# Low parts of the first weight groups and of the shifted operand, and the rotations of keys and queries, issued on VectorE instead of GpSimd

## The chip, the cores and the metric

The kernel runs on one core of a Trainium2 chip. The metric is the device time of one execution in microseconds (us). A core has five engines, each with its own queue of instructions: TensorE (PE in the rows; its weight loads are PEld), VectorE (DVE), ScalarE (ACT), GpSimd (POOL) and SyncE (SP), which issues most of the DMAs.

## The reference, cut to what matters

One step of a hybrid encoder layer, for a prompt of 1024 frames and a sample of 64 frames with 512 cached ones, in float32. The input is normalized, scaled and shifted by the conditioning vector; one combined projection feeds two mixers, a latent attention and a gated linear recurrence; their outputs go through an output projection, and an MLP follows.

```python
h = rms_norm(x, g_norm1) * (1 + scale1) + shift1
proj = h @ w_in
c_q, c_kv, k_rope_raw, gq, gk, gv, g_lr, g_r = jnp.split(proj, split_points, axis=-1)
# latent attention: q and k get a per-head RMS norm, then the last 64 columns are rotated
q = jnp.concatenate([q[..., :QK_NOPE], rope(q[..., QK_NOPE:], q_pos)], axis=-1)
k = jnp.concatenate([k[..., :QK_NOPE], rope(k[..., QK_NOPE:], k_pos)], axis=-1)
# rope, on the halves x1, x2 of the 64 columns:
concatenate([x1 * cos - x2 * sin, x2 * cos + x1 * sin])
# gated linear recurrence over chunks of 64 frames (gla_recurrence)
x = x + gate1 * (concatenate([a_out, b_out]) @ w_out)
h2 = rms_norm(x, g_norm2) * (1 + scale2) + shift2
x = x + gate2 * (square(relu(h2 @ w_up)) @ w_down)
```

## The kernel before

**Products.** Each float32 operand of a large product is split into a high part, a rounded copy that ScalarE casts, and a low part, the operand minus the high part. `mm3` (L93 to L95) then makes three products: high by high, and each high by the other's low part. `split` (L101, L102) makes both parts of an operand; the engine of the subtraction is its last argument. In names, `hh` and `hl` are the high and low part of the normalized input `hf`, `wh` and `wl` those of a weight group, which arrives in a buffer `raw`.

**Tiling and stages.** The 1088 frames lie along the columns, in three chunks of 384, 384 and 320; the 1024 features lie along 8 tiles of 128 partitions, indexed by `k` or `kt`. At the start, `scales` sums the squares of a chunk (L331) and scales `hf` with the result (L379). The weight groups A0 and A1 (columns of the recurrence's queries and keys) come first, in eight units of 128x512, and `split_first` (L309) makes their low parts. `qk` multiplies chunk after chunk with A0 and A1 into `gqk` (L498, L508). `shifts` adds the shift to `hf`: for an even `k`, ScalarE writes `hh` (L478) and VectorE `hl` (L479); for an odd `k`, VectorE adds the shift in place (L476) and `split` makes both parts. Two later groups of weights, B0 and B1, are split at L213 and L105 in units of 128x528; when a low part is done its `raw` is free for the load of a later unit. L511 and L514 add the shift's share to `gqk`.

The recurrence follows (L560 to L800 or so): per tile of 128 frames TensorE transposes at L573, VectorE computes gates and sums, and GpSimd products of decays and operands at L660, L668 and L706. Then comes the latent attention: `keys_values` makes normalized keys and values for 13 tiles of frames, `queries` the queries for 9, and `attend` the attention. Tables of cosines and sines, `tabk` and `tabq` (`rotary_table`), are loaded and scaled at L824. In `keys_values` the raw rotary key is multiplied by both halves of the table into `ra` and `rt` and combined into `R`; the low part `kl` (L888) and the rotated keys `kr` (L895) follow transpositions on TensorE. `queries` forms products `qa` and `qt`, combines them into `qr` (L926, L927), and transposes `qn` (L938) and `qr` (L945). Powers for the norms run on GpSimd (L121, L351, L877, L930).

**What sets the order.** The stages are generators that yield an estimated cost and a condition, and `interleave` takes turns among them; from the order in which instructions are issued that way, a scheduler makes the queue of each engine. Each engine then runs its queue strictly in order, and waits on semaphores for data and for buffers. So an instruction that goes to another engine can also move its neighbours in several queues.

Of the kernel before, what the change touches and what calls it, by code (L numbers as in the profile page):

```python
# [36 lines left out]
def f32(ap):  # L37
    return ap.bitcast(F32)
# [33 lines left out]
def layer(ctx: ExitStack, tc: tile.TileContext, I, O):  # L72
# [202 lines left out]
    with ExitStack() as sctx:  # L275
# [26 lines left out]
        LO = ((DVE, POOL), (POOL, POOL))  # L302

        def split_first(hf, j):
            for u in (2 * hf, 2 * hf + 1):
                wh, wl = groups[GROUPS[j][0]]
                hi, lo, raw = wh[:, 2 * u:2 * u + 2], wl[:, 2 * u:2 * u + 2], first.pop((j, u))
                mm = ACT.copy(hi, raw)
                m2 = LO[hf][j].tensor_tensor(out=lo, in0=raw, in1=f32(hi), op=ALU.subtract)  # L309
                if hf == 0:  # L310
                    tc.keep_in_program_order(mm)
                    tc.keep_in_program_order(m2)
            done.add(f"half {hf} {j}")
# [7 lines left out]
        def scales(c):  # L321
# [8 lines left out]
            for n in (4, 2, 1):  # L330
                mm = (POOL if n == 4 and c == 2 else DVE).tensor_tensor(out=sq[:, 0:n, :cn], in0=sq[:, 0:n, :cn],  # L331
                                                                   in1=sq[:, n:2 * n, :cn], op=ALU.add)
                if c == 0:
                    tc.keep_in_program_order(mm)
# [125 lines left out]
        def shifts():  # L460
# [8 lines left out]
            for c in range(3):  # L469
                c0, cn = CHUNKS[c]  # L470
                yield 2000, 0, has(f"qk {c}")
                for k in range(KT):
# [8 lines left out]
                    if k % 2:  # L481
                        split(h["h"][:, k, c0:c0 + cn], h["l"][:, k, c0:c0 + cn], hf[:, k, c0:c0 + cn], POOL)
# [338 lines left out]
    def rotary_table(tab, w):  # L821
        SP.dma_start(tab, I["k_rope_tab"].rearrange("p t (c d) -> p t c d", d=64))
        t = tab.rearrange("p t c d -> p (t c) d")
        POOL.tensor_tensor(out=t, in0=t, in1=grow[:, w:w + 1].broadcast_to([P, 16, 64]), op=ALU.mult)  # L824
# [23 lines left out]
    def keys_values(lh, ll, ki, tab, n, kv, slot):  # L848
# [8 lines left out]
        POOL.tensor_tensor(out=a[:n, 0], in0=kraw[:n, ki], in1=tabk[:n, tab, 0], op=ALU.mult)  # L857
        POOL.tensor_tensor(out=t_[:n, 0], in0=kraw[:n, ki], in1=tabk[:n, tab, 1], op=ALU.mult)
        DVE.tensor_tensor(out=R[:n, 0, :, 0:32], in0=a[:n, :, 0:32].broadcast_to([n, 2, 32]),
                          in1=t_[:n, :, 32:64].broadcast_to([n, 2, 32]), op=ALU.subtract)  # L860
        POOL.tensor_tensor(out=R[:n, 0, :, 32:64], in0=a[:n, :, 32:64].broadcast_to([n, 2, 32]),
                           in1=t_[:n, :, 0:32].broadcast_to([n, 2, 32]), op=ALU.add)
# [37 lines left out]
    def queries(i, ch, cl_, n, tab):  # L900
# [26 lines left out]
        POOL.tensor_tensor(out=qr[:n, :, :, 32:64], in0=half(a, 32), in1=half(t_, 0), op=ALU.add)  # L927
# [915 lines left out]
```

## Time and profile before

| what | value |
|---|---|
| median of 3 runs | 1406.49 us (1406.09 to 1408.61) |
| profiled execution, its own time | 1403.91 us |
| its span in the trace | 1402.1 us |
| TensorE busy | 1340.1 us, 96% |
| VectorE busy | 890.4 us, 64% |
| ScalarE busy | 656.1 us, 47% |
| GpSimd busy | 183.8 us, 13% |

The span runs from the first to the last instruction that the profiler recorded in one execution; positions in the rows below are us from its start. A busy share says how much of the span an engine worked, not whether somebody waited for it; for that the rows give the idle time ahead of an instruction in brackets, with what ended it.

### The profile page before, as it was taken

To read this page: it belongs to the slowest core of one execution; us is meant where nothing else is said; L and a number is where in the kernel's file an instruction comes from. 1 tells how busy PE (TensorE), PEld (TensorE's weight loads), DVE (VectorE), ACT (ScalarE), POOL (GpSimd) and SP (SyncE) were. 2 spreads that over 40 slices of the span, in tenths; PEclk is the share of its full clock that TensorE was granted. 3 is DMA by queue.
4 is the path that set the end of the run, shared out by engine and by line. 5 is a ranking of instruction groups with operands and counts; after the bars stand their busy time and mean duration, and the time that the engine had idled before them with its cause. 6 is when DMAs were issued, how large, how long until landed. Compare 5 with 4: busy or idle time off the path is not lost.

```text
span 1402.1 us, 26363 instructions
## 1 busy us (share of the span) xinstructions
PE 1340.1 (96%) x10014; PEld 1254.8 (89%) x10014; DVE 890.4 (64%) x1965; ACT 656.1 (47%) x1623; POOL 183.8 (13%) x317
## 2 busy tenths in 40 slices
PE   6988889997999999999999999999999999999998
PEld 5888778886876778899998999999999999999998
DVE  5688777336546665665689766566555866774554
ACT  5465454334326565563386454454444343433342
POOL 3155445213122220100000000000000000000000
PEclk9999999999999999999999999999999999999999
DMA  9320021384344532073324543443348764543440
GB/s 345 115 73 9 16 73 47 112 238 120 100 130 124 172 108 77 26 219 115 107 85 135 191 158 133 140 158 133 112 157 285 280 227 152 188 122 97 126 128 33
DMA packets 165592, 188.15 MB, mean 134 GB/s; under 512 B 16814, under 2 KB 116442, under 8 KB 165466
## 3 DMA queue, kind: packets, MB, share of 16 engines
q1 hardware_dynamic: 158010, 180.90, 40.3%
q10 hardware_dynamic: 7456, 5.57, 1.2%
q8 instruction: 79, 1.29, 0.4%
q14 instruction: 47, 0.39, 0.1%
HBM read 132.97 MB, written 53.46 MB: 133 GB/s over the span
## 4 chain that ended last, share of the span: by engine, by line
PE 78%; DVE 10%; DMA 4%; ACT 3%; POOL 2%; issue 2%; SPq 0%; DVEq 0%; POOLq 0%; ACTq 0%
PE mm L93 13%; PE mm L94 13%; PE mm L95 13%; PE g L95 5%; PE g L93 5%; PE g L94 5%; PE mm L964 3%; PE tp L93 3%; PE tp L95 3%; PE tp L94 3%; PE g L991 2%; PE mm L166 2%; DMA raw<-in_w_in 1%; PE tp L1001 1%; DVE ST L725 1%
## 5 line engine op out<-in xcount | busy, mean ns | idle before, releaser
L101 ACT CAST opers<-quad 128x512 fp32r<-128x512 f32 x112 | 69.5, 620 | 184.5 <-PE mm L95 146.8
L102 DVE TENSOR_TENSOR opers<-quad,opers 128x512 fp32r<-128x512 f32 x112 | 77.3, 690 | 114.5 <-ACT opers L101 114.5
L95 PE MATMUL mm<-opers 128*128 128x272 f32 x448 | 128.9, 288 | 0.0
L93 PE MATMUL mm<-opers 128*128 128x272 f32 x448 | 128.5, 287 | 0.3 <-DVE e L1775 0.3
L94 PE MATMUL mm<-opers 128*128 128x272 f32 x448 | 128.3, 286 | 0.0
L93 PE MATMUL mm<-ah,wh 128*128 128x272 f32 x424 | 122.2, 289 | 3.3 <-ACT wh L101 2.2
L94 PE MATMUL mm<-al,wh 128*128 128x272 f32 x424 | 121.5, 287 | 0.0
L95 PE MATMUL mm<-ah,wl 128*128 128x272 f32 x424 | 121.4, 288 | 0.0
L93 PE MATMUL mm<-hh,wh 128*128 128x384 f32 (+2 forms) x264 | 90.6, 346 | 0.7 <-ACT hh L101 0.7
L94 PE MATMUL mm<-hl,wh 128*128 128x384 f32 (+2 forms) x264 | 87.6, 333 | 0.0
L95 PE MATMUL mm<-hh,wl 128*128 128x384 f32 (+2 forms) x264 | 87.2, 331 | 0.0
L93 PEld LDWEIGHTS mm<-opers 128*128 128x128 f32 x448 | 84.7, 189 | 0.5 <-issue 0.5
L95 PEld LDWEIGHTS mm<-opers 128*128 128x128 f32 x448 | 84.2, 188 | 0.0
L94 PEld LDWEIGHTS mm<-opers 128*128 128x128 f32 x448 | 84.0, 188 | 0.0
L93 PEld LDWEIGHTS mm<-ah,wh 128*128 128x128 f32 x424 | 79.8, 188 | 4.4 <-ACT wh L101 2.6
L94 PEld LDWEIGHTS mm<-al,wh 128*128 128x128 f32 x424 | 79.7, 188 | 0.0
L95 PEld LDWEIGHTS mm<-ah,wl 128*128 128x128 f32 x424 | 79.5, 188 | 0.0
L102 DVE TENSOR_TENSOR opers<-ru,opers 128x544 fp32r<-128x544 f32 x108 | 77.7, 720 | 2.2 <-ACT opers L101 2.0
L101 ACT CAST opers<-ru 128x544 fp32r<-128x544 f32 x108 | 69.4, 643 | 13.1 <-PE mm L95 11.7
L101 ACT CAST wh<-ru 128x512 fp32r<-128x512 f32 x67 | 41.3, 617 | 67.5 <-PE g L94 24.5
L102 DVE TENSOR_TENSOR wl<-ru,wh 128x512 fp32r<-128x512 f32 x67 | 46.1, 691 | 36.3 <-ACT wh L101 36.0
L93 PE MATMUL mm<-wh,hh 128*128 128x264 f32 (+3 forms) x216 | 66.0, 306 | 1.6 <-ACT wh L213 1.6
(410 smaller groups left out, 4370.0 us busy)
## 6 DMA issues: line engine op xcount, KB each, us to landing
ru<-u_d SPq DMA_DIRECT2D x108, 272.0 KB, 2.8
raw<-in_w_ada SPq DMA_DIRECT2D x40, 512.0 KB, 3.9
ru<-in_w_up SPq DMA_DIRECT2D x32, 512.0 KB, 4.0
quad<-in_w_down SPq DMA_DIRECT2D x16, 1024.0 KB, 6.5
u_d<-st SPq DMA_DIRECT2D x60, 272.0 KB, 2.1
u_d<-sc SPq DMA_DIRECT2D x45, 272.0 KB, 2.2
raw<-in_w_in SPq DMA_DIRECT2D x22, 256.0 KB, 3.5
x<-in_xo_T SPq DMA_DIRECT2D x8, 544.0 KB, 5.2
```

What stands on the lines that cost most here:

```text
L93: PE.matmul(out, lhsT=ah, rhs=bh, start=first, stop=False, skip_group_check=more)
L94: PE.matmul(out, lhsT=ah, rhs=bl, start=False, stop=False, skip_group_check=more)
L95: PE.matmul(out, lhsT=al, rhs=bh, start=False, stop=last, skip_group_check=more)
L101: ACT.copy(hi, src)
L102: eng.tensor_tensor(out=lo, in0=src, in1=f32(hi), op=ALU.subtract)
L166: mm = PE.matmul(acc[32 * j:32 * j + 32, 0:256], lhsT=scT[:, k, :], rhs=was[k][:, 256 * j:256 * (j + 1)], start=(k == 0), stop=(k == KT - ...
L725: DVE.copy_predicated(ST[:n, :, :n].rearrange("p c (b r h) -> p c b r h", r=2, h=hf)[:, :, :, 1], masks[:n, mlv, :n // 2].rearrange("p (o ...
L964: PE.matmul(sp[:n, :w], lhsT=x[:, hd, :n], rhs=y[:, hd, :w], start=(j == 0), stop=(j == 4))
L991: PE.matmul(op[:n, 0:P], lhsT=pt[:kw, k, :n], rhs=kvs[kt // 4].v[:kw, kt % 4, hd], start=(kt == 0), stop=(kt == nkt - 1))
L1001: PE.transpose(tp[:kw, k, :n], pr[k0 // 4][:n, P * k:P * k + kw], ident[:n, :n])
```

## The change

Instructions of six kinds, all on GpSimd before, are issued on VectorE: the low parts of A0 and A1 that were GpSimd's (six of eight, L309); the first addition of squares of chunk 2 (L331); the low parts of the shifted operand for odd `k` (twelve, at L102); the scaling of both rotary tables (L824); three of the four instructions that rotate a key tile (L857, L858, L861); and the second half of a rotated query tile (L927). On GpSimd stay the products of the recurrence and the powers. The arithmetic is the same. Two lines go, so that what is line N before is line N - 2 after, from L303 on.

```diff
--- before.py
+++ after.py
@@ -299,14 +299,12 @@
                     _, a, b = GROUPS[j]
                     SP.dma_start(first[j, u], w_in_cols(a, b)[2 * u * P:2 * u * P + 2 * P].rearrange("(k p) n -> p k n", p=P))
 
-        LO = ((DVE, POOL), (POOL, POOL))
-
         def split_first(hf, j):
             for u in (2 * hf, 2 * hf + 1):
                 wh, wl = groups[GROUPS[j][0]]
                 hi, lo, raw = wh[:, 2 * u:2 * u + 2], wl[:, 2 * u:2 * u + 2], first.pop((j, u))
                 mm = ACT.copy(hi, raw)
-                m2 = LO[hf][j].tensor_tensor(out=lo, in0=raw, in1=f32(hi), op=ALU.subtract)
+                m2 = DVE.tensor_tensor(out=lo, in0=raw, in1=f32(hi), op=ALU.subtract)
                 if hf == 0:
                     tc.keep_in_program_order(mm)
                     tc.keep_in_program_order(m2)
@@ -328,7 +326,7 @@
                     tc.keep_in_program_order(mm)
             yield 600, 1000, None
             for n in (4, 2, 1):
-                mm = (POOL if n == 4 and c == 2 else DVE).tensor_tensor(out=sq[:, 0:n, :cn], in0=sq[:, 0:n, :cn],
+                mm = DVE.tensor_tensor(out=sq[:, 0:n, :cn], in0=sq[:, 0:n, :cn],
                                                                    in1=sq[:, n:2 * n, :cn], op=ALU.add)
                 if c == 0:
                     tc.keep_in_program_order(mm)
@@ -479,7 +477,7 @@
                             DVE.scalar_tensor_tensor(out=h["l"][:, k, a:b], in0=x, scalar=s1, in1=f32(h["h"][:, k, a:b]),
                                                      op0=ALU.add, op1=ALU.subtract)
                     if k % 2:
-                        split(h["h"][:, k, c0:c0 + cn], h["l"][:, k, c0:c0 + cn], hf[:, k, c0:c0 + cn], POOL)
+                        split(h["h"][:, k, c0:c0 + cn], h["l"][:, k, c0:c0 + cn], hf[:, k, c0:c0 + cn], DVE)
                     yield 0, 300, None
 
         def qk():
@@ -821,7 +819,7 @@
     def rotary_table(tab, w):
         SP.dma_start(tab, I["k_rope_tab"].rearrange("p t (c d) -> p t c d", d=64))
         t = tab.rearrange("p t c d -> p (t c) d")
-        POOL.tensor_tensor(out=t, in0=t, in1=grow[:, w:w + 1].broadcast_to([P, 16, 64]), op=ALU.mult)
+        DVE.tensor_tensor(out=t, in0=t, in1=grow[:, w:w + 1].broadcast_to([P, 16, 64]), op=ALU.mult)
 
     rotary_table(tabk, 1)
 
@@ -854,12 +852,12 @@
         a = kw.tile([P, 1, 64], F32, name="ra")
         t_ = kw.tile([P, 1, 64], F32, name="rt")
         ACT.activation(t_[:n, 0], kraw[:n, ki], AF.Square, accum_out=ss[:n, 8:9])
-        POOL.tensor_tensor(out=a[:n, 0], in0=kraw[:n, ki], in1=tabk[:n, tab, 0], op=ALU.mult)
-        POOL.tensor_tensor(out=t_[:n, 0], in0=kraw[:n, ki], in1=tabk[:n, tab, 1], op=ALU.mult)
+        DVE.tensor_tensor(out=a[:n, 0], in0=kraw[:n, ki], in1=tabk[:n, tab, 0], op=ALU.mult)
+        DVE.tensor_tensor(out=t_[:n, 0], in0=kraw[:n, ki], in1=tabk[:n, tab, 1], op=ALU.mult)
         DVE.tensor_tensor(out=R[:n, 0, :, 0:32], in0=a[:n, :, 0:32].broadcast_to([n, 2, 32]),
                           in1=t_[:n, :, 32:64].broadcast_to([n, 2, 32]), op=ALU.subtract)
-        POOL.tensor_tensor(out=R[:n, 0, :, 32:64], in0=a[:n, :, 32:64].broadcast_to([n, 2, 32]),
-                           in1=t_[:n, :, 0:32].broadcast_to([n, 2, 32]), op=ALU.add)
+        DVE.tensor_tensor(out=R[:n, 0, :, 32:64], in0=a[:n, :, 32:64].broadcast_to([n, 2, 32]),
+                          in1=t_[:n, :, 0:32].broadcast_to([n, 2, 32]), op=ALU.add)
         kr = kw.tile([P, H, P], F32, name="krt", bufs=1)
         for g in range(2):
             pk = g_bank()
@@ -924,7 +922,7 @@
             return t[:n, :, o:o + 32].rearrange("p h (o c) -> p h o c", o=1).broadcast_to([n, H, 2, 32])
 
         DVE.tensor_tensor(out=qr[:n, :, :, 0:32], in0=half(a, 0), in1=half(t_, 32), op=ALU.subtract)
-        POOL.tensor_tensor(out=qr[:n, :, :, 32:64], in0=half(a, 32), in1=half(t_, 0), op=ALU.add)
+        DVE.tensor_tensor(out=qr[:n, :, :, 32:64], in0=half(a, 32), in1=half(t_, 0), op=ALU.add)
         POOL.tensor_scalar(out=ss[:n, 4:8], in0=ss[:n, 0:4], scalar1=192.0 / 192 ** 2, scalar2=epsq[:n, i:i + 1],
                            op0=ALU.mult, op1=ALU.add)
         POOL.tensor_tensor(out=ss[:n, 4:8], in0=ss[:n, 4:8], in1=mhalf[:n], op=ALU.pow)
```

The scheduler places the moved instructions, and others with them, in a new order. ScalarE's queue is shown where TensorE goes from chunk 0 to chunk 1 of the first projection (- before, + after; `sq` are squares for the scale, `gqk` copies of a product, `hh` casts of the operand):

```order
-L326 ACTIVATE sq<-hf 128x4x320 x2
-L498 ACTIVATE gqk<-mm 128x384
-L101 CAST hh<-hf 128x384 x2
-L498 ACTIVATE gqk<-mm 128x384
-L101 CAST hh<-hf 128x384 x6
-L508 ACTIVATE gqk<-mm 128x384 x2
+L324 ACTIVATE sq<-hf 128x1536
+L101 CAST hh<-hf 128x384
+L496 ACTIVATE gqk<-mm 128x384 x2
+L324 ACTIVATE sq<-hf 128x4x320 x2
+L496 ACTIVATE gqk<-mm 128x384 x2
+L101 CAST hh<-hf 128x384 x8
```

Before, two of chunk 1's eight casts stood ahead of the fourth copy of `gqk`; now all eight stand behind it.

VectorE's queue in the shift stage, around the first low parts of B0, before:

```order
L511 TENSOR_SCALAR add<-mm 128x2
L479 SCALAR_TENSOR_TENSOR hl<-hf,modT,hh 128x384
L514 TENSOR_SCALAR gqk<-gqk,add 128x768
L476 TENSOR_SCALAR hf<-hf,modT 128x64
L476 TENSOR_SCALAR hf<-hf,modT 128x256
L476 TENSOR_SCALAR hf<-hf,modT 128x64
L476 TENSOR_SCALAR hf<-hf,modT 128x256
L476 TENSOR_SCALAR hf<-hf,modT 128x64
L105 TENSOR_TENSOR wl<-raw,wh 128x528 x2
L511 TENSOR_SCALAR add<-mm 128x2
```

and after:

```order
L474 TENSOR_SCALAR hf<-hf,modT 128x384
L102 TENSOR_TENSOR hl<-hf,hh 128x384
L512 TENSOR_SCALAR gqk<-gqk,add 128x768
L102 TENSOR_TENSOR hl<-hf,hh 128x384
L509 TENSOR_SCALAR add<-mm 128x2
L105 TENSOR_TENSOR wl<-raw,wh 128x528
L512 TENSOR_SCALAR gqk<-gqk,add 128x768
L509 TENSOR_SCALAR add<-mm 128x2
L105 TENSOR_TENSOR wl<-raw,wh 128x528
L512 TENSOR_SCALAR gqk<-gqk,add 128x768
L105 TENSOR_TENSOR wl<-raw,wh 128x528
```

The low parts of B0 moved ahead of the shifts of chunk 2 (columns 64 and 256), five of which stood ahead of the first low part before; the subtractions for odd `k` (L102) are now in this queue.

VectorE's queue at the first query tile, of 64 frames, before:

```order
L911 COPY qn<-g 64x384
L845 TENSOR_TENSOR cql<-cqr,cqh 128x384
L888 SCALAR_TENSOR_TENSOR kl<-tp,vT,kh 128x4x128
L920 TENSOR_TENSOR qa<-qn,tabq 64x256
L921 TENSOR_TENSOR qt<-qn,tabq 64x256
L895 TENSOR_TENSOR kr<-tp,kr 64x4x128
L926 TENSOR_TENSOR qr<-qa,qt 64x8x32
L940 SCALAR_TENSOR_TENSOR ql<-tp,vT,qh 128x4x64
```

and after:

```order
L909 COPY qn<-g 64x384
L843 TENSOR_TENSOR cql<-cqr,cqh 128x384
L822 TENSOR_TENSOR tabq<-tabq,grow 128x1024
L886 SCALAR_TENSOR_TENSOR kl<-tp,vT,kh 128x4x128
L918 TENSOR_TENSOR qa<-qn,tabq 64x256
L919 TENSOR_TENSOR qt<-qn,tabq 64x256
L893 TENSOR_TENSOR kr<-tp,kr 64x4x128
L924 TENSOR_TENSOR qr<-qa,qt 64x8x32
L925 TENSOR_TENSOR qr<-qa,qt 64x8x32
L938 SCALAR_TENSOR_TENSOR ql<-tp,vT,qh 128x4x64
```

The scaling of the query's table now stands ahead of the key's low part `kl`, and the second half of `qr` directly behind the first.

## Rows read from the trace of the kernel before

**Rows 1.** Profile page: span, and busy time of each engine (share of the span) and instructions.

```profile
span 1402.1 us, 26363 instructions
...
PE 1340.1 (96%) x10014; PEld 1254.8 (89%) x10014; DVE 890.4 (64%) x1965; ACT 656.1 (47%) x1623; POOL 183.8 (13%) x317
```

**Rows 2.** Stretches: length, busy us of PE, PEld, DVE, ACT, POOL; clock, DMA share, GB/s.

```profile
25.80:66.00 40.20, 40.20 (x258) 33.93 (x259) 27.43 (x61) 18.89 (x34) 9.87 (x8) 1.00 0.55 182
66.00:90.00 24.00, 21.47 (x146) 20.80 (x146) 23.28 (x48) 17.56 (x44) 11.59 (x12) 1.00 0.19 56
112.00:245.00 133.00, 117.08 (x796) 105.15 (x796) 105.31 (x324) 65.99 (x231) 69.00 (x126) 0.99 0.13 37
```

**Rows 3.** Timeline, shift stage: start, us, engine, line, instruction, [idle before, what ended it].

```profile
81.56 1.32 DVE L105 TENSOR_TENSOR wl<-raw,wh 128x528 fp32r<-128x528 f32 x2
...
84.24 0.28 PE L94 MATMUL mm<-wl,hh 128*128 128x264 f32 x1
84.36 0.28 PE L95 MATMUL mm<-wh,hl 128*128 128x264 f32 x1
...
86.22 0.39 PE L93 MATMUL mm<-wh,hh 128*128 128x264 f32 x1 [1.58 <-ACT wh L213]
...
87.48 0.39 PE L94 MATMUL mm<-wl,hh 128*128 128x264 f32 x1 [0.87 <-DVE wl L105]
```

**Rows 4.** Timeline at the first query tile.

```profile
407.92 0.75 DVE L888 SCALAR_TENSOR_TENSOR kl<-tp,vT,kh 128x512 fp32r<-128x512 f32 x1
...
408.25 2.38 POOL L824 TENSOR_TENSOR tabq<-tabq,grow 128x1024 f32<-128x1024 f32 x1 [1.00 <-DMA tabq<-in_k_rope_tab]
...
408.73 0.46 PE L938 MATMUL tp<-ident,qn 64*128 64x64 f32 x4 [0.34 <-DVE kl L888]
...
412.54 0.71 POOL L927 TENSOR_TENSOR qr<-qa,qt 64x256 f32<-64x256 f32 x1
...
413.31 0.46 PE L945 MATMUL tp<-ident,qr 64*128 64x64 f32 x4 [2.28 <-POOL qr L927]
```

**Rows 5.** Timeline of the start, up to chunk 1's first cast.

```profile
16.24 1.29 DVE L309 TENSOR_TENSOR wl<-raw,wh 128x512 fp32r<-128x512 f32 x2
...
21.52 1.49 DVE L102 TENSOR_TENSOR hl<-hf,hh 128x384 fp32r<-128x384 f32 x3
...
41.51 0.33 PE L93 MATMUL mm<-hh,wh 128*128 128x384 f32 x1
...
41.70 0.49 ACT L498 ACTIVATE gqk<-mm 128x384 f32<-128x384 f32 x1
...
42.09 0.50 ACT L101 CAST hh<-hf 128x384 fp32r<-128x384 f32 x1
```

**Rows 6.** GpSimd's groups, 66 to 90 us: count | busy us, mean ns | idle before.

```profile
L102 POOL TENSOR_TENSOR hl<-hf,hh 128x384 fp32r<-128x384 f32 x8 | 8.2, 1047 | 15.4 <-ACT hh L101 15.4
L102 POOL TENSOR_TENSOR hl<-hf,hh 128x320 fp32r<-128x320 f32 x4 | 3.4, 861 | 6.9 <-ACT hh L101 6.8
```

**Rows 7.** VectorE's groups of the same stretch.

```profile
L479 DVE SCALAR_TENSOR_TENSOR hl<-hf,modT,hh 128x384 fp32r<-128x384 f32 x8 | 6.5, 825 | 0.0
L476 DVE TENSOR_SCALAR hf<-hf,modT 128x384 f32<-128x384 f32 x8 | 5.5, 717 | 0.0
```

**Rows 8.** Timeline of VectorE, shift stage, single instructions with GpSimd idle beside them.

```profile
67.35 0.42 DVE L476 TENSOR_SCALAR hf<-hf,modT 128x384 f32<-128x384 f32 x1
...
77.20 0.60 DVE L479 SCALAR_TENSOR_TENSOR hl<-hf,modT,hh 128x384 fp32r<-128x384 f32 x1
```

**Rows 9.** DMA issues, 55 to 100 us: KB each, median us to landing.

```profile
raw<-in_w_in SPq DMA_DIRECT2D x8, 264.0 KB, 2.8
```

**Rows 10.** Timeline of VectorE in one key tile.

```profile
331.00 0.23 DVE L859 TENSOR_TENSOR R<-ra,rt 128x64 f32<-128x64 f32 x1 [0.90 <-POOL rt L858]
331.18 0.75 DVE L888 SCALAR_TENSOR_TENSOR kl<-tp,vT,kh 128x512 fp32r<-128x512 f32 x1
```

**Rows 11.** GpSimd's waits, 0 to 470 us: total us, times, longest.

```profile
POOL rt L858 <- ACT rt L856: 25.6, 8, 12.2
```

## The prediction

> **What bounds the kernel now.** I read the share of busy time first, then the stages, then TensorE's waits stage by stage, then the other engines at each wait. TensorE is busy for 1340.1 of the 1402.1 us span [rows 1], so a change on VectorE or GpSimd counts only where it moves one of TensorE's waits, which come to 62 us in all. The table by stage [rows 2] shows where they are not: from 25.8 to 66 us TensorE is busy for all of 40.20 us, so anything that holds it there is a pure loss, and nothing there can be gained. From 66 to 90 us, while the shift is added to the operand, it waits for 2.53 us; VectorE is busy for 23.28 of these 24 us and is what is waited for. From 112 to 245 us, the recurrence, it waits for 16 us, but there the change leaves every instruction where it was. Two waits stand at the end of the shift stage: 1.58 us for a high part `wh` and 0.87 us for a low part `wl`, both of the last unit of weight group B0 [rows 3]; that is 2.45 us of the 2.53. In the latent attention the only long wait that an edited line sets is 2.28 us for the first rotated query, `qr` of L927 [rows 4].
>
> The profiled execution took 1403.91 us, 1.8 us more than its span; the median of the runs shown is 1406.49, that is 2.6 above it. I sum changes against the profiled execution and add them to the median.
>
> **Term 1, the start: +1.3 us.** Six low parts of 128x512 go from GpSimd to VectorE, whose own two take 1.29 us, 0.65 each [rows 5]. Two of them fill a gap ahead of the first scale. The other four stand between VectorE's instructions for the second half of the first chunk, 4 x 0.65 = 2.6 us, and the addition of squares of chunk 2 (1280 columns; from 0.50 for 384 and 0.65 for 512 columns an estimate of 1.5 us) stands ahead of the first L379 of chunk 1. I worked VectorE's queue through with these prices: the last high and low parts of chunk 0 come within 0.1 to 0.2 us of TensorE's need, so I charge 0.2 us. The rest comes from ScalarE, by the rows shown of its order: the fourth copy of `gqk` now stands ahead of the first cast of chunk 1. Before, the first cast ran ahead of it, TensorE took chunk 1 at 41.51, and the copy ran from 41.70, released by the last product of chunk 0; the cast behind it started at 42.09 and took 0.50 [rows 5]. Now chunk 1's first cast is that next one, ends at 42.59 and holds TensorE for 42.59 - 41.51 = 1.1 us. A later start of chunk 1's first L379 by about 1 us is hidden under this wait; without that cover it would cost about 0.8. Nothing can be gained here, since TensorE waits for nothing before. Bounds 0.5 (half of the wait filled by other products) and 2.0 (the four low parts cost 0.9 more); taken 1.3. What follows is counted from TensorE's own times, so this delay is carried on and not absorbed.
>
> **Term 2, the shift stage: -0.3 us.** Twelve subtractions leave GpSimd, where they took 8.2 and 3.4 us [rows 6]. On VectorE a 384-column one takes 0.50 (three in 1.49 [rows 5]), so eight of them, and four of 320 columns at five sixths of that, add about 5.6 us. Against it: VectorE's own 384-column instructions take 0.825 and 0.717 us on average while GpSimd works beside them [rows 7], and 0.60 and 0.42 where it stands idle [rows 8]. That is 8 x 0.225 + 8 x 0.30 = 4.2 us given back, and up to 7.8 if narrower ones lose in the same measure. VectorE's stage becomes between 1.4 us longer and 2.2 us shorter. More matters in the order: the first low part of B0 came at 81.56 [rows 3], behind five shifts of chunk 2, and now comes ahead of all of chunk 2. Ahead of it on VectorE, from 67.35 [rows 8], stand 8 x 0.60 + 8 x 0.42 + 8 x 0.50 = 12.2 us, somewhat less where neighbours overlap, and some 1 us of small ones: it starts between 79 and 80.5. Its buffer then frees earlier for the last unit's load, which takes 2.8 us to land [rows 9]; with 0.7 for the low part that frees it and as much for the cast, both by the 0.69 or so that a low part of this size takes (two in 1.32 [rows 3]), the high part is there between 83.2 and 84.7. TensorE wants it at 86.22 - 1.58 = 84.64, so the wait of 1.58 goes. The last low part is the queue's: I put its end at 85.0 to 85.7, so TensorE takes it at 85.75 in place of 87.48, a gain of 1.7.
>
> Most of that is not kept. TensorE's order now has 10 more projection products (0.12 us each, from 84.24 to 84.36 [rows 3], so 1.2 us) ahead of the transposition L573 that opens the recurrence, and as many fewer behind it, where TensorE waits for the chain of the first tile anyway. So L573 comes 0.5 us earlier, not 1.7, and VectorE's copy for tile 1 now stands ahead of tile 0's gates and may wait for its product: +0.2. Net -0.3; bounds -1.7 (all kept) and +0.9 (the copy holds the gates by a whole product more).
>
> On [rows 7, 8] bears a rule of the Trainium skill ("SBUF — State Buffer", Who interferes with whom): VectorE and GpSimd share one port pair, and an instruction that needs it while the other has it is held until that other one ends. The trace agrees as far as 0.42 against 0.717 goes. By the rule the whole 11.6 us of GpSimd's subtractions could have been VectorE's loss; then VectorE gains 11.6 - 5.6 = 6 us there and the stage's wait of 2.45 goes entirely, and the sum below would be -1.6 in place of +0.5. What it would do is rival A.
>
> **Term 3, the keys: +0.3 us.** Thirteen tiles, three instructions each. On VectorE a 64-column one takes 0.23 [rows 10], so some 0.6 to 0.7 us a tile, 9 us in all. They cost little because VectorE had to wait for GpSimd's part before: 0.90 us idle ahead of L859, until 331.00, and then `kl` at 331.18 [rows 10]. Now L858, L859 and L861 stand in that gap and `kl` comes 0 to 0.1 us later. L858 waits for ScalarE's square, which writes the same tile; queued behind it on VectorE is `kl`, for which TensorE's next transposition waits. Without the gap a tile would cost 0.6. Bounds -0.5 (the idle of 0.9 was worth something) and +1.3 (0.1 for each tile).
>
> **Term 4, the first query: -0.8 us.** The query's table is scaled on GpSimd from 408.25 for 2.38 us, after 1.00 us of waiting for its load; L920 and L921 on VectorE read it [rows 4]. On VectorE 1024 columns are an estimate of 1.2 us (0.65 for 512 [rows 5], twice the columns). It stands ahead of `kl` in the order, so `kl` goes from 407.92 to about 409.4, and the transposition L938 that waited for it goes from 408.73 to about 410.1: +1.4. Behind it follow two products of 0.4, `kr` of 0.6 and two sums of 0.4 (estimates between the 0.23 for 64 columns [rows 10] and the 0.65 for 512): both halves of `qr` are there at 412.2 in place of 412.54 + 0.71, and TensorE, with 413.31 - 2.28 - 408.73 = 2.3 us of other products after L938, takes L945 at 412.45 in place of 413.31. Bounds -2.3 (the whole wait) and +0.5 (the load lands later and holds `kl`). The eight further queries put 0.4 us each on VectorE beside TensorE's products of the same tile, which hide them; uncovered they would cost 3.4. The key table (1.2 us) I cost at nothing: it is read only when the keys begin, behind the recurrence, and VectorE has idle time until then; uncovered it would cost 1.2.
>
> **Sum.** 1.3 - 0.3 + 0.3 - 0.8 = +0.5: 1403.9 becomes 1404.4, and against the median 1407.0.
>
> **Rivals.**
> A, faster: the relief of the port reaches TensorE whole. Both waits of [rows 3] go and are not given back in the recurrence, and the 2.28 of the first query goes: 1.1 - 2.45 - 2.28 = -3.6, 1402.9. For it: the stretched VectorE rows. Against: 16 us of chain-bound waiting right behind, and the table that comes ahead of `kl`. It decides if L573 comes over 1.5 us earlier, counted from the shift's transposition.
> B, slower: VectorE stands still for ScalarE. GpSimd waited 25.6 us, in 8 waits of up to 12.2, for the square that L858 overwrites [rows 11]; VectorE now has that wait in its queue, ahead of `kl`. As soon as it exceeds the 0.9 us that VectorE idled before, each tile pays; 0.3 on each of 13 gives 3.9 on top of the sum: 1410.9. Against: most of GpSimd's wait was time in which it had come early.
> C: the edits are hidden altogether, the start too, since other products fill its wait: 1406.5.
>
> **How the numbers follow.** The forecast has 0.42, C 0.13, A 0.23, B 0.22. A change of 0.2% (2.8 us) is about what a measurement of this kernel can tell from none. The forecast and C lie within it (0.55), A below (0.23), B above (0.22). The bounds of the terms add to -4.0 and +4.7: 1402.5 to 1411.2. That is the range; it takes in the forecast with C and more than half of A and of B, so under 2 in 10 is left out.
>
> **What would show it.** Right: TensorE waits about 1.1 us for a cast `hh` near 41.5; the wait for B0's high part is gone and that for its low part is about 1 us; L938 waits over 1 us and L945 hardly; `kl` of the keys within 0.1 us of before. Wrong: no wait at the start; VectorE idle over 1 us a tile ahead of L858; a recurrence that starts over 1 us earlier or later than TensorE's delay explains.

## The result: 0.6% faster, below the forecast's range

The changed kernel takes 1399.9 us (median of 6 runs, 1397.72 to 1400.85), the kernel before 1407.36 (6 runs, 1406.09 to 1408.61); the ratio is 0.9939, with a 95% interval of 0.9928 to 0.9949. That is faster by 7 to 10 us. Forecast were 1407.0 and a range of 1402.5 to 1411.2.

The profile page of the changed kernel, beside [rows 1]: VectorE is busy for 9 us more, GpSimd for 50 us less, and TensorE has the same work in a shorter span.

```profile
span 1398.3 us, 26315 instructions
...
PE 1340.3 (96%) x10014; PEld 1258.9 (90%) x10014; DVE 899.3 (64%) x2034; ACT 654.3 (47%) x1623; POOL 134.3 (10%) x248
```

The same stretches as the first two of [rows 2], with the same columns: the loss and the gain that the prediction looked for are both there.

```profile
25.80:66.00 40.20, 39.22 (x255) 33.37 (x256) 29.29 (x68) 18.29 (x33) 2.10 (x3) 1.00 0.54 181
66.00:90.00 24.00, 24.00 (x172) 23.90 (x171) 23.00 (x61) 18.65 (x46) 0.00 (x0) 1.00 0.21 57
```

At the start TensorE now waits 0.98 us; in the shift stage its 2.53 us of waiting are gone altogether, and it begins 172 products there where it began 146. The next fence is the timeline of the start, to be read beside [rows 5]: the fourth copy of `gqk`, the first casts of chunk 1 behind it, and TensorE's wait for them.

```profile
41.63 0.49 ACT L496 ACTIVATE gqk<-mm 128x384 f32<-128x384 f32 x1 [1.61 <-PE mm L95]
...
42.01 1.33 ACT L101 CAST hh<-hf 128x384 fp32r<-128x384 f32 x3
...
42.57 0.44 PE L93 MATMUL mm<-hh,wh 128*128 128x384 f32 x1 [0.98 <-ACT hh L101]
```

VectorE's groups in the shift stage (66 to 90 us; instructions, then busy us and mean ns of one), beside [rows 6, 7]. GpSimd does nothing there now, and VectorE's own instructions of 384 columns fell from 825 to 614 ns and from 717 to 415.

```profile
L477 DVE SCALAR_TENSOR_TENSOR hl<-hf,modT,hh 128x384 fp32r<-128x384 f32 x8 | 4.8, 614 | 0.0
L102 DVE TENSOR_TENSOR hl<-hf,hh 128x384 fp32r<-128x384 f32 x8 | 4.4, 556 | 0.1
...
L474 DVE TENSOR_SCALAR hf<-hf,modT 128x384 f32<-128x384 f32 x8 | 3.3, 415 | 0.0
```

The timeline at the end of that stage, beside [rows 3]: the first and the last low part of B0, and TensorE's first product with the last one. It stands without a wait.

```profile
79.37 0.70 DVE L105 TENSOR_TENSOR wl<-raw,wh 128x528 fp32r<-128x528 f32 x1
...
85.76 0.70 DVE L105 TENSOR_TENSOR wl<-raw,wh 128x528 fp32r<-128x528 f32 x1
...
86.52 0.39 PE L94 MATMUL mm<-wl,hh 128*128 128x264 f32 x1
```

And the first query tile, beside [rows 4]; everything is 2.6 us earlier by then. The table is scaled in 1.23 us, `kl` follows it, and TensorE takes `qn` and `qr` without a wait ahead of either.

```profile
405.24 1.23 DVE L822 TENSOR_TENSOR tabq<-tabq,grow 128x1024 f32<-128x1024 f32 x1
406.38 0.75 DVE L886 SCALAR_TENSOR_TENSOR kl<-tp,vT,kh 128x512 fp32r<-128x512 f32 x1
...
407.18 0.46 PE L936 MATMUL tp<-ident,qn 64*128 64x64 f32 x4
...
408.87 0.41 DVE L925 TENSOR_TENSOR qr<-qa,qt 64x256 f32<-64x256 f32 x1
...
409.95 0.46 PE L943 MATMUL tp<-ident,qr 64*128 64x64 f32 x4
```

To see where time is won and kept, I compare the starts of TensorE's n-th product in two traces (10014 products in each). The table is worked out from the traces; each kernel was profiled a second time, unedited (below). Entries are us, negative where the first-named is ahead.

```
product n                       300    400    740    850   1500   2400   2500   3000   3100  10000
start in before, us            49.6   64.1  119.3  136.5  243.7  402.9  423.3  497.2  512.8 1396.3
after - before               +1.15  +0.42  -1.09  -2.53  -2.29  -2.59  -6.27  -4.70  -5.49  -3.55
second trace of each         +0.94  +0.22  -2.82  -4.25  -3.91  -5.93  -7.72  -6.16  -6.95  -7.13
shifted operand only - before -0.16  -0.16  -1.97  -3.40  -3.13  -3.46  -3.21  -3.18  -3.18  -0.56
tables only - before          +0.30  +0.31  +1.86  +1.85  +3.43  +2.87  -0.67  -0.71  -0.71  +1.83
tables and queries - before   +0.09  +0.09  +1.64  +0.21  +0.22  +1.85  -1.60  +0.08  -0.69  +2.16
```

Two steps are won in both pairs, by product 850 and between products 2400 and 2500; a small one lies between 3000 and 3100. The rest of the movement is mostly TensorE's clock, which each trace shows at half (1.2 of 2.4 GHz, a granted clock of 0.5) in a few short stretches, not always the same ones; part of the first two steps is the clock too, as the sections below show. The first trace of before has none between 700 and 780 us (granted clock 1.00, as in one other trace of the thirteen here, 0.94 to 0.98 in the others); so its 1403.91 us lie under its own median, and the last column of the first pair understates the gain.

### The profile page after: what moved, and what is told of

Its sections match the earlier page's. It is cut to its first block, busy times and chain, and to the rows that moved or that the text cites. A ratio compares the mean times of both kernels' runs of the same rounds, so it can differ in the third digit from the quotient of the medians.

```text
span 1398.3 us, 26315 instructions
## 1 busy us (share of the span) xinstructions
PE 1340.3 (96%) x10014; PEld 1258.9 (90%) x10014; DVE 899.3 (64%) x2034; ACT 654.3 (47%) x1623; POOL 134.3 (10%) x248
## 4 chain that ended last, share of the span: by engine, by line
PE 81%; DVE 9%; DMA 4%; ACT 3%; POOL 2%; issue 2%; SPq 0%; ACTq 0%; DVEq 0%; POOLq 0%
PE mm L93 14%; PE mm L95 13%; PE mm L94 13%; PE g L93 6%; PE g L95 6%; PE g L94 6%; PE mm L962 3%; PE tp L93 3%; PE tp L95 3%; PE tp L94 3%; PE g L989 3%; PE mm L166 2%; DMA raw<-in_w_in 1%; PE tp L999 1%; DVE ST L723 1%
## 5 line engine op out<-in xcount | busy, mean ns | idle before, releaser
L102 DVE TENSOR_TENSOR opers<-quad,opers 128x512 fp32r<-128x512 f32 x112 | 77.2, 689 | 114.5 <-ACT opers L101 114.5
L102 DVE TENSOR_TENSOR opers<-ru,opers 128x544 fp32r<-128x544 f32 x108 | 77.5, 719 | 2.2 <-ACT opers L101 2.0
L102 DVE TENSOR_TENSOR wl<-ru,wh 128x512 fp32r<-128x512 f32 x67 | 45.9, 689 | 36.5 <-ACT wh L101 36.3
```

What stands on the lines that cost most here:

```text
L102: eng.tensor_tensor(out=lo, in0=src, in1=f32(hi), op=ALU.subtract)
```

## The experiments

My theory after reading the traces: the gain is made at two places, the shift stage and the first query, because GpSimd's work there had stretched or delayed what TensorE waits for; start and keys weigh nothing. Rivals: the gain is the keys'; it is only the new order of the queues; it is only the clock. Ratios below are to runs of the kernel before taken beside them, with their 95% intervals.

**Each part alone.** Four kernels make one part of the change and leave the rest as before.

The shifted operand alone:

```diff
-                        split(h["h"][:, k, c0:c0 + cn], h["l"][:, k, c0:c0 + cn], hf[:, k, c0:c0 + cn], POOL)
+                        split(h["h"][:, k, c0:c0 + cn], h["l"][:, k, c0:c0 + cn], hf[:, k, c0:c0 + cn], DVE)
```

> Only the twelve subtractions of the shifted operand (L102 for odd k) go to VectorE. Theory: GpSimd's reads stretched VectorE there, and the low parts of B0 come earlier in the new order, so both TensorE waits of the shift stage (1.58 for wh, 0.87 for wl) go and TensorE is 2.5 to 3.2 us earlier at 90 us; 1.1 to 2.5 us of it is kept through the recurrence: median 1.1 to 2.5 us under that of before. Rival, the forecast's own term: most is given back in the recurrence, -0.3. Rival, the clock: no change of the median, whatever the one trace shows.

Measured: 1403.59 us, 0.9966 (0.9954 to 0.9979), that is 4.8 us (3.0 to 6.5). TensorE is 3.2 us ahead at product 600 (95 us), 1.97 at product 740 and 3.13 at the end of the recurrence; the last figure has a half-clock stretch of before in it (120.6 to 124.0 us). The theory's place is right; it is more than the 1.1 to 2.5 expected of the median, and the term of -0.3 falls.

Tables and queries alone:

```diff
-        POOL.tensor_tensor(out=t, in0=t, in1=grow[:, w:w + 1].broadcast_to([P, 16, 64]), op=ALU.mult)
+        DVE.tensor_tensor(out=t, in0=t, in1=grow[:, w:w + 1].broadcast_to([P, 16, 64]), op=ALU.mult)
...
-        POOL.tensor_tensor(out=qr[:n, :, :, 32:64], in0=half(a, 32), in1=half(t_, 0), op=ALU.add)
+        DVE.tensor_tensor(out=qr[:n, :, :, 32:64], in0=half(a, 32), in1=half(t_, 0), op=ALU.add)
```

> Only the two rotary tables (L824) and the queries' second half (L927) go to VectorE. Theory: the query's table no longer waits in GpSimd's queue behind the key tile's rotations, so the 2.28 us wait at the first query goes whole, with nothing lost at kl: TensorE 2.3 us earlier at 420 us, and up to 0.9 more at 500 us; median 2.3 to 3.3 us lower. Rival, the forecast's own term: the table holds kl and TensorE's transposition of qn, 0.8 us gained in all.

Measured: 1404.23 us, 0.9964 (0.9952 to 0.9977), 5.1 us (3.2 to 6.8). The step between products 2400 and 2500 is 3.5 us against the first trace of before, which runs at half clock there, and 1.5 against the second, which does not; 0.8 more comes between 3000 and 3100.

The start alone:

```diff
-                m2 = LO[hf][j].tensor_tensor(out=lo, in0=raw, in1=f32(hi), op=ALU.subtract)
+                m2 = DVE.tensor_tensor(out=lo, in0=raw, in1=f32(hi), op=ALU.subtract)
...
-                mm = (POOL if n == 4 and c == 2 else DVE).tensor_tensor(out=sq[:, 0:n, :cn], in0=sq[:, 0:n, :cn],
+                mm = DVE.tensor_tensor(out=sq[:, 0:n, :cn], in0=sq[:, 0:n, :cn],
```

> Only the first low parts (L309) and the first addition of squares of chunk 2 (L331) go to VectorE. Theory: chunk 1's first cast stands behind the fourth gqk copy and TensorE waits about 1.0 us near 41.5; 0.7 of it is won back where a later wait for hh was, so +0.4 at 90 us and +0.4 of the median. Rival, the forecast's own term: +1.3 to the end.

Measured: 1407.8 us, 0.9997 (0.9986 to 1.0007): nothing that can be told from zero. In the trace TensorE is 1.31 us late at product 300 and 0.58 at product 400, as expected in size, but what wins 0.7 back is not a later wait for `hh`, as I had written. Before, the products of the modulation (L166) ran between the others in a group of 2 (from 49.84 to the next product at 50.39) and one of 6 (51.48 to 52.04); here they run as one group of 8, from 51.15 to 51.72. A group takes some 0.56 us whatever its number, and 0.75 with the wider spacing of its neighbours (0.27 and 0.29 us, where the products otherwise follow each other at 0.18), so one group less wins the 0.73.

The keys alone:

```diff
-        POOL.tensor_tensor(out=a[:n, 0], in0=kraw[:n, ki], in1=tabk[:n, tab, 0], op=ALU.mult)
-        POOL.tensor_tensor(out=t_[:n, 0], in0=kraw[:n, ki], in1=tabk[:n, tab, 1], op=ALU.mult)
+        DVE.tensor_tensor(out=a[:n, 0], in0=kraw[:n, ki], in1=tabk[:n, tab, 0], op=ALU.mult)
+        DVE.tensor_tensor(out=t_[:n, 0], in0=kraw[:n, ki], in1=tabk[:n, tab, 1], op=ALU.mult)
...
-        POOL.tensor_tensor(out=R[:n, 0, :, 32:64], in0=a[:n, :, 32:64].broadcast_to([n, 2, 32]),
-                           in1=t_[:n, :, 0:32].broadcast_to([n, 2, 32]), op=ALU.add)
+        DVE.tensor_tensor(out=R[:n, 0, :, 32:64], in0=a[:n, :, 32:64].broadcast_to([n, 2, 32]),
+                          in1=t_[:n, :, 0:32].broadcast_to([n, 2, 32]), op=ALU.add)
```

> Only the keys' rotations (L857, L858, L861) go to VectorE. Theory: they stand where VectorE waited for GpSimd, so -0.3 to +0.3 of the median. Rival: the keys hold a good part of the gain, since 13 tiles each lose a wait: -2 or more, most of it between 270 and 500 us. Rival, slower: VectorE stands still for ScalarE's square, +2 or more.

Measured: 1408.43 us, 0.9994 (0.998 to 1.0008). The second rival falls: VectorE waits for ScalarE's square twice, 2.8 us in all, and nothing is lost by it that can be told. The first is not excluded by the interval, which reaches to -2.8 us, but the trace has no gain there: TensorE is 0.07 us ahead at product 1500 and 0.15 at product 2400. The four ratios multiply to 0.9921, and the whole change has 0.9939 (0.9928 to 0.9949): within the intervals the parts add.

**Contention or order, in the shift stage.** The changed kernel keeps its order on every engine, and GpSimd gets twelve subtractions beside it whose result nobody reads.

```diff
+            shade = xp.tile([P, 320], F32, name="shade", bufs=1)
...
                         split(h["h"][:, k, c0:c0 + cn], h["l"][:, k, c0:c0 + cn], hf[:, k, c0:c0 + cn], DVE)
+                        POOL.tensor_tensor(out=shade, in0=hf[:, k, c0:c0 + 320],
+                                           in1=f32(h["h"][:, k, c0:c0 + 320]), op=ALU.subtract)
```

> The changed kernel, with twelve more subtractions of 128x320 on GpSimd in the shift stage, of the operands that GpSimd read there before, into a tile that nobody reads (extra work; every other queue keeps its order). Theory, contention: VectorE's 384-column instructions go from 0.42 and 0.61 back to 0.7 and 0.8 us, its stage gets 4 us longer, a wait of TensorE for B0's parts of 1 to 3 us comes back, and 1.5 to 3.5 us of the gain are lost: ratio to before 0.996 to 0.9975. Rival, order: what counted was that B0's low parts moved ahead of chunk 2's shifts; GpSimd's work beside them changes nothing at TensorE: ratio 0.994 as for the change.

Measured: 1407.89 us, 0.9996 (0.9987 to 1.0004): the whole gain is lost. TensorE is 4.7 us behind the changed kernel at product 600, and 6.0 at product 850, with a half-clock stretch from 117.5 us in between. On TensorE, VectorE and ScalarE the trace has the same sequence of operations as the changed kernel's, and no other engine waits for GpSimd's extra work. VectorE's groups of that kernel from 66 to 90 us, then GpSimd's:

```profile
L102 DVE TENSOR_TENSOR hl<-hf,hh 128x384 fp32r<-128x384 f32 x8 | 6.5, 826 | 0.0
L478 DVE SCALAR_TENSOR_TENSOR hl<-hf,modT,hh 128x384 fp32r<-128x384 f32 x8 | 6.3, 794 | 0.0
L105 DVE TENSOR_TENSOR wl<-raw,wh 128x528 fp32r<-128x528 f32 x4 | 3.8, 958 | 0.0
L475 DVE TENSOR_SCALAR hf<-hf,modT 128x384 f32<-128x384 f32 x8 | 3.3, 408 | 0.0
```

```profile
L482 POOL TENSOR_TENSOR shade<-hf,hh 128x320 f32<-128x320 f32 x9 | 8.5, 941 | 25.5 <-ACT hh L101 19.2 <-issue 6.0 <-POOL shade L482 0.2
```

TensorE's waits of that kernel from 66 to 92 us (total, times, longest):

```profile
PE mm L94 <- DVE wl L105: 2.9, 4, 1.4
PE mm L93 <- ACT wh L213: 0.4, 1, 0.4
```

With the order unchanged, only GpSimd's work can have brought the waits back, so order alone is not the gain. Size and kind were off: I expected 1.5 to 3.5 us of loss, and the addition in place (L475) stays at 408 ns, while the operations with two inputs go from 556 to 826, from 614 to 794 and from 700 to 958. VectorE now carries the subtractions as well, and without the relief the move would be a loss, 4.7 - 2.8 = 1.9 us at product 600 against the kernel before. What the new order adds to the relief stays open: no run takes GpSimd's work away and keeps the old order.

**What made the first query late.** Only the tables go to VectorE (the first edit of tables and queries); the second half of `qr` stays on GpSimd.

> Only the two rotary tables (L824) go to VectorE; the second half of the query (L927) stays on GpSimd. Theory: the table in GpSimd's queue was what made the first query late, so the wait of 2.28 us falls to 0.5 us or less and the ratio is 0.997 to 0.9985, nearly that of tables and queries together. Rival: GpSimd's half of the query (0.71 us behind two operations for the norm) held it: the wait keeps over 1 us, ratio over 0.9985.

Measured: 1403.56 us, 0.9967 (0.9955 to 0.9979), a little more than expected; as much as with the queries' half within the intervals. TensorE waits ahead of neither transposition, though GpSimd still makes half of `qr`:

```profile
412.78 0.46 PE L938 MATMUL tp<-ident,qn 64*128 64x64 f32 x4
...
414.75 0.46 PE L945 MATMUL tp<-ident,qr 64*128 64x64 f32 x4
```

So it was the table's scaling on GpSimd that held the query: 2.38 us there for 1.23 on VectorE, with two operations for the norm and the half of `qr` queued behind it. Its place behind the key tile's rotations, which I had named as the reason for tables and queries, has no part: GpSimd stood idle for 1.00 us ahead of the table, until its load had landed [rows 4]. With the keys alone on VectorE none of these rotations stands ahead of it; it starts at 408.00 for 408.25, and the query still waits 2.19 us:

```profile
408.00 2.39 POOL L824 TENSOR_TENSOR tabq<-tabq,grow 128x1024 f32<-128x1024 f32 x1 [3.94 <-DMA tabq<-in_k_rope_tab]
```

The 0.8 us between products 3000 and 3100 are missing here (-0.71 at both) and come with the queries' half, but through TensorE's order: two groups of modulation products become one, as at the start. The timeline of before, then of the changed kernel:

```profile
500.19 0.62 PE L166 MATMUL mm<-raw,scT 128*32 128x256 f32 x2
...
505.48 0.63 PE L166 MATMUL mm<-raw,scT 128*32 128x256 f32 x6
```

```profile
495.42 0.64 PE L166 MATMUL mm<-raw,scT 128*32 128x256 f32 x8
```

In return the changed kernel has one group more between products 2400 and 2500 (4 for 3).

**Is there a better version?** All but the start, and then also without the keys.

```diff
 (the change, with these as before)
-                m2 = DVE.tensor_tensor(out=lo, in0=raw, in1=f32(hi), op=ALU.subtract)
+                m2 = LO[hf][j].tensor_tensor(out=lo, in0=raw, in1=f32(hi), op=ALU.subtract)
...
-                mm = DVE.tensor_tensor(out=sq[:, 0:n, :cn], in0=sq[:, 0:n, :cn],
+                mm = (POOL if n == 4 and c == 2 else DVE).tensor_tensor(out=sq[:, 0:n, :cn], in0=sq[:, 0:n, :cn],
```

> The whole change but the start: the first low parts (L309) and the first addition of squares of chunk 2 (L331) stay on GpSimd. Theory: TensorE's wait of about 1.0 us near 41.5 is gone and nothing else moves, so TensorE is 0.4 to 0.6 us ahead of the changed kernel from 90 us on: ratio to before about 0.9935, at most 0.9945. Rival: GpSimd's use of the memory beside VectorE costs as much at the start as it does in the shift stage, so it is no faster than the changed kernel or slower, ratio over 0.995.

Measured: 1400.88 us, 0.9943 (0.9929 to 0.9957). In the trace TensorE is 0.3 us ahead of the changed kernel at product 400, as the theory has it; by product 1500 it is 0.5 behind, with half-clock stretches at other places (110.7 and 192.6 us, for 172.3 in the changed kernel). In the time nothing can be told, and the interval leaves the rival in.

For the second, the keys' three lines too stand as before.

> Two parts of the change together: the shifted operand's subtractions, and the tables with the queries' second half; start and keys stay on GpSimd. Theory: the two gains lie in different stages and add, -0.34% and -0.36%: ratio 0.993, and no slower than the whole change (0.9939). Rival: they overlap, because what TensorE gains early it waits for later: 0.995 or more.

Measured: 1399.59 us, 0.9942 (0.9922 to 0.9963): the two parts make up the whole change. Whether all of both gains is kept (their ratios multiply to 0.9930) or a little is lost can't be told from the interval. No version is measurably faster than the change itself.

**The clock.** In the first trace of before, TensorE runs at half clock from 414 us on, right behind the query's wait; the changed kernel does not there. Two rows by stretch, of before; the first is its half-clock stretch behind the shift stage, the second the one at the query (behind the counts: granted clock, DMA share, GB/s):

```profile
120.50:124.00 3.50, 3.50 (x19) 3.50 (x19) 2.10 (x7) 2.70 (x15) 1.32 (x4) 0.52 0.01 2
...
414.00:417.60 3.60, 3.60 (x13) 0.95 (x11) 2.19 (x6) 1.62 (x10) 1.34 (x2) 0.53 0.02 5
```

I put the wait back into the changed kernel, without the table: the second half of the first query on GpSimd, seven times over.

```diff
-        DVE.tensor_tensor(out=qr[:n, :, :, 32:64], in0=half(a, 32), in1=half(t_, 0), op=ALU.add)
+        for _ in range(7 if n == 64 else 1):
+            (POOL if n == 64 else DVE).tensor_tensor(out=qr[:n, :, :, 32:64], in0=half(a, 32), in1=half(t_, 0), op=ALU.add)
```

> The changed kernel, with the second half of the first query tile back on GpSimd and issued seven times there (extra work of some 5 us, the same values each time), so that TensorE's transposition of that tile waits again, 1.5 to 2.5 us near 411. Theory: a wait of that length at this place is followed by a stretch in which TensorE is granted half its clock, as in the four traces that have the wait of 2.2 to 2.5 us (half clock from 410.6 to 414.4 on) and in none of the six that lack it; so TensorE loses the wait and some 1.5 us behind it, 3 to 4 us by 425, and a stretch at 1.2 GHz begins between 411 and 416. Rival: where the half clock falls has nothing to do with the wait; only the wait itself is lost, 1.5 to 2.5 us, and no such stretch begins before 440.

Measured: 1404.96 us, 0.9976 (0.9967 to 0.9985), 3.4 us over the median of the changed kernel's runs taken beside it (1401.57, below). The wait is back, and the half clock behind it; the timeline, then the row of that stretch:

```profile
413.63 0.46 PE L944 MATMUL tp<-ident,qr 64*128 64x64 f32 x4 [2.65 <-POOL qr L926]
```

```profile
414.20:417.80 3.60, 3.60 (x15) 2.14 (x10) 1.94 (x4) 0.57 (x3) 1.34 (x2) 0.53 0.50 143
```

TensorE loses 4.8 us by product 2500 (from 0.56 ahead to 4.23 behind), 2.65 of them the wait; 0.9 us comes back by product 3000, where the changed kernel has a stretch at half clock near 445 (0.95 over 425 to 460 us) and this one has none (1.00). The theory holds at its place, and the net price is less than wait and clock together. That is no single case: of the seven traces without the query's wait, five have half clock somewhere from 445 to 459 us, and of the five with half clock at the query one has.

Then both kernels once more, unedited.

> The changed kernel once more, unedited, for a second trace. Theory: the stretches at half clock between 85 and 125 and at 411 to 418 are missing again, because the waits ahead of them are. Rival, chance: they stand elsewhere in this trace, some of them in these two places.

Measured: 1401.57 us, 0.9947 (0.993 to 0.9963). No half clock from 405 to 425, but one between 85 and 130.

> The kernel before once more, unedited, for a second trace. Theory: a stretch at half clock between 88 and 125 and one at 413 to 415 stand in it again, as in every trace with those waits; ratio 1.000. Rival, chance: one of them is missing.

Measured: 1407.73 us, 1.0001 (0.999 to 1.0011). A half clock between 85 and 125 again, but none behind the query's wait, which is there:

```profile
417.08 0.46 PE L945 MATMUL tp<-ident,qr 64*128 64x64 f32 x4 [1.89 <-POOL qr L927]
```

So "missing again" falls at the first place and "in every trace" at the second. The mean granted clock of all traces in two stretches (half-clock stretches lower it to 0.91 to 0.96):

| traces | 85 to 130 us | 405 to 425 us |
|---|---|---|
| with the waits of both places: before (2 traces), start alone, keys alone | 0.96, 0.92, 0.96, 0.96 | 0.91, 1.00, 0.91, 0.91 |
| with the shift stage's waits: tables alone, tables and queries | 0.92, 0.96 | 1.00, 1.00 |
| with the query's wait: shifted operand alone, query made late | 1.00, 1.00 | 0.91, 0.91 |
| with neither: change (2 traces), all but the start, two parts | 1.00, 0.96, 0.96, 0.96 | 1.00, 1.00, 1.00, 1.00 |
| changed kernel with GpSimd's extra subtractions | 0.96 | 1.00 |

At the query, half clock stands behind five of six waits and in none of seven traces without one. Behind the shift stage all seven traces with its waits have it, but so have three of the six without.

## Why the prediction was wrong

**What bounds the kernel** was right: the start, the shift stage and the first query are where TensorE's time changed, and the keys did nothing. Rival A is the case that came, its -3.6 close to the -3.8 that the waits and the order come to below. The sign that was to decide for it did not show: L573 over 1.5 us earlier, counted from the shift's transposition, where it was 0.8 to 1.4 us (from VectorE's L181, which follows that transposition, to L573: 30.97 us before; 30.15, 29.78 and 29.57 in the three traces with the whole change up to there). The sum was 8 us off, and these are its steps.

**Term 1, the start (+1.3).** The mechanism was right to 0.1 us: a wait of 0.98 for the cast `hh` behind the fourth `gqk` copy, where 1.1 was forecast. What is left of it at product 400 is 0.42 and 0.22 us in the two pairs and 0.58 with the start alone, since the step "this delay is carried on and not absorbed" left out that the new order also merges two groups of modulation products.

**Term 2, the shift stage (-0.3).** VectorE's own instructions of 384 columns gave back 8 x 0.211 + 8 x 0.302 = 4.1 us for 4.2 forecast, the first low part of B0 came at 79.37 (between 79 and 80.5), the last one ended at 86.46 (85.0 to 85.7 forecast, ahead of 0.4 us of the start's delay). The narrower ones and the addition to `gqk` gave back 4 x (0.149 + 0.106 + 0.265 + 0.134) = 2.6 us more, which the prediction had only as its bound. VectorE's groups from 66 to 90 us, before and then after:

```profile
L514 DVE TENSOR_SCALAR gqk<-gqk,add 128x768 f32<-128x768 f32 x4 | 3.1, 764 | 0.0
L479 DVE SCALAR_TENSOR_TENSOR hl<-hf,modT,hh 128x256 fp32r<-128x256 f32 x4 | 2.3, 582 | 0.0
L479 DVE SCALAR_TENSOR_TENSOR hl<-hf,modT,hh 128x64 fp32r<-128x64 f32 x4 | 2.2, 541 | 0.0
L476 DVE TENSOR_SCALAR hf<-hf,modT 128x64 f32<-128x64 f32 x4 | 1.5, 380 | 0.0
```

```profile
L512 DVE TENSOR_SCALAR gqk<-gqk,add 128x768 f32<-128x768 f32 x4 | 2.5, 615 | 0.0
L477 DVE SCALAR_TENSOR_TENSOR hl<-hf,modT,hh 128x256 fp32r<-128x256 f32 x4 | 1.9, 476 | 0.0
L477 DVE SCALAR_TENSOR_TENSOR hl<-hf,modT,hh 128x64 fp32r<-128x64 f32 x4 | 1.1, 276 | 0.0
L474 DVE TENSOR_SCALAR hf<-hf,modT 128x64 f32<-128x64 f32 x4 | 1.0, 246 | 0.0
```

So VectorE got 6.7 us back. The twelve subtractions took it 5.4 us, from the start of each to the start of the next (their records overlap by some 0.08 us and add to 6.4): its stage became about 1 us shorter. L573 came 0.4 us earlier, 97.35 for 97.74, with 0.4 of the start's delay in it, so 0.8 by itself, where 0.5 was forecast.

What failed is the next step: that most of the gain "is not kept", because the 10 more products ahead of L573 are missing behind it "where TensorE waits for the chain of the first tile anyway". They were kept. At product 740, where neither first trace has run at half clock yet, the change is 1.09 us ahead in spite of 0.42 lost at the start: 1.5 us, near the 0.4 and the 10 products at 0.12. The shifted operand alone has 1.97 there. Nor does the recurrence take it back: the lead of 2.29 us at product 1500 has 1.4 in it that before loses by its half clock at 120.6 us (by product 850), and lacks some 0.2 that the changed kernel loses by its own at 172.3 (by product 1500), so 1.1 of it is the stage's. This was near the bound of -1.7 that the term gave as "all kept". The wait of about 1 us that was to stay for B0's last low part did not come either, with 15 more products ahead of it (555 for 540).

By the rule of the Trainium skill that the prediction weighed ("SBUF — State Buffer", Who interferes with whom), the whole of GpSimd's 11.6 us could have been VectorE's loss. The traces agree in kind, less in size: VectorE got 6.7 us back, and in the experiment with extra subtractions the stretch is 8 x 0.270 + 8 x 0.180 + 4 x 0.258 = 4.6 us in three groups beside 8.5 us of GpSimd.

**Term 3, the keys (+0.3).** Right as far as can be told: 0.9994 (0.998 to 1.0008).

**Term 4, the first query (-0.8).** Again the marked instruction was right: L945 was forecast at 412.45, and it came at 409.95 with everything 2.6 us earlier, which is 412.5 in the time of before. But 12 more products stand ahead of it in the new order (2454 for 2442), so TensorE's wait did not just shrink, it was filled. And the wait of over 1 us for `kl` at L938 did not come, for the same reason: `kl` is late by 1.1 us, where 1.5 was forecast, but the 5 products put ahead of L938 (2436 for 2431) cover it. Without a half-clock stretch the step is 1.8 us (the second pair, products 2400 to 2500); with the 0.8 between products 3000 and 3100, a merging of modulation products for which the forecast had no term, it is 2.6 for 0.8.

The failing step is one and the same in terms 2 and 4: **I read the gain from the time at which a marked instruction starts**, and dismissed or did not count the work that the new order puts ahead of it. Work ahead of a mark is work done, if TensorE does not wait longer behind it.

**The clock was not in the sum.** Over the timed runs, the mean granted clock is 0.990 for before (64 runs), 0.989 to 0.990 for start and keys alone, 0.991 for the shifted operand, 0.992 for tables alone and for tables and queries, and 0.992 and 0.993 for the change (two times 6 runs). Among the runs of before, 0.001 of clock goes with 1.0 to 1.4 us of time; so, as an estimate from these runs, 0.002 to 0.003 account for 2 to 4 of the 7.5 us. The waits and the order, at +0.3 - 1.5 - 2.6 = -3.8, account for the rest. At the query the half clock comes with the wait in five of six traces, and was brought back with it. For the shift stage the cause of the clock's difference stays open: waits and half clock go together there only in part, and no experiment took the one without the other.

The median that the sum was added to stood on three runs, 1406.49; six give 1407.36 and 23 later ones 1407.93. That is luck in the forecast's favour: from 1407.36 it would have been 1407.9, and the miss 8.0 us in place of 7.1.

## What to carry to other kernels

Where a change lets a scheduler reorder TensorE, don't read the gain from when one marked instruction starts: count the products ahead of it in both orders, and take the wait that is left. An engine that works beside VectorE on the same operands should be costed by what it does to all of VectorE's rows, the narrow ones too: here moving the work over cost VectorE 5.4 us and gave back 6.7 in one stage. And a wait of TensorE can cost somewhat more than itself, by the half clock that often follows: one of 2.65 us, put back, cost 3.4.

## What the runs showed of the hardware

A wait of 1.9 to 2.7 us at the first query was followed by a stretch at half clock in five of six traces (13 and 15 products in 3.6 us in the two shown); nothing like it stood there in seven traces without the wait. With the tables alone, whose trace lacks both wait and half clock there, the time was 4.6 us lower (3.0 to 6.3); the wait put back, 2.65 us, raised it by 3.4. How much of this is the clock at this place can't be told from the medians, since a stretch at half clock between 445 and 459 us comes more often without the wait.

GpSimd's subtractions do not slow VectorE's instructions evenly: a single one either keeps its time or takes some 0.4 to 0.6 us more. In the kernel with the extra subtractions, the timeline of VectorE and of GpSimd shows it:

```profile
78.11 0.61 DVE L478 SCALAR_TENSOR_TENSOR hl<-hf,modT,hh 128x384 fp32r<-128x384 f32 x1
78.64 0.41 DVE L475 TENSOR_SCALAR hf<-hf,modT 128x384 f32<-128x384 f32 x1
...
78.97 1.10 DVE L478 SCALAR_TENSOR_TENSOR hl<-hf,modT,hh 128x384 fp32r<-128x384 f32 x1
...
78.88 0.78 POOL L482 TENSOR_TENSOR shade<-hf,hh 128x320 f32<-128x320 f32 x1 [1.44 <-ACT hh L101]
```

The same operation takes 0.61 us alone and 1.10 when it starts 0.09 us after one of GpSimd's that ends at 79.66. The addition in place of 384 columns kept its 0.41 in this kernel, where it ran beside GpSimd for at most 0.17 us of it; in the kernel before it took 1.02 where it lay under one whole, hence the mean of [rows 7].

Between larger products, a group of modulation products (L166) takes TensorE 0.55 us with 2 of them, 0.56 with 6 and 0.57 with 8. Two of them merged into one made up 0.73 us at the start and 0.8 between products 3000 and 3100.
